# One five-block tile per pair of weight blocks, and a masked bias with the row maximum in one instruction, in a three-branch decoder layer

## The chip, the cores and the metric

One Trainium2 core of eight is used. It has a matrix engine (TensorE, PE in the profile; its weight loads are PEld), VectorE (DVE), ScalarE (ACT), GpSimd (POOL), SyncE (SP), which here only issues transfers, and 16 DMA engines. The metric is the device time of one execution in microseconds.

## The reference

The layer takes x of 512 tokens by 1024 channels, in float32, and computes one mixer with three branches:

```
h = rmsnorm(x) * norm_g;  proj = h @ w_in           # 1024 -> some 14,000 columns, split by name
A: q,k = silu(conv4(aq)), silu(conv4(ak))            # 4 heads of 256, mLSTM with gates ai, af
   yA = rmsnorm(mlstm(q, k, av, ai, af)) * ml_norm_g * sigmoid(ao) * silu(az)
B: 8 heads of 128, forgetting attention:
   F = cumsum(log_sigmoid(bf));  s = q.k/sqrt(128) + F[query] - F[key], -inf above the diagonal
   yB = softmax(s) @ bv * silu(bz)
C: yC = (windowed means of cu (2,4,8,16 tokens) - cu) @ pool_w * pool_scale * silu(cz)
merged = sum over branches of sigmoid(g_n) * (y_n @ w_branch_n)
out = rmsnorm(x + merged @ w_out) * final_g
```

## The kernel before, in words

Every product is made in float32 quality from three passes: a weight or an activation is split into `hi` (a rounded copy, made on ACT, `hi_of`, L288) and `lo` (the rest, made on DVE, `lo_of`, L291), and `mm3` (L300 to L302) adds hi.hi, hi.lo and lo.hi. So each weight block passes through DMA, then ACT, then DVE, before PE can use it.

The weights come in an order written by `plan()`, in two kinds. A **unit** (U) is one block of 128 x 1024 elements (512 KB) and gives 24 matmuls. A **pair** (P) is two blocks of output columns made together by a Strassen-like scheme with seven instead of eight products (`pair`, seven calls of `prod`, 84 matmuls). For a pair, four parts of weights are wanted: part 0 (the two halves of the first block), part 1 (one half of the second), and parts 2 and 3, which are sums of blocks. The first layer head, the first two groups of gates, `av`, `bv`, `pw` (the pool weights), `wb` (branches) and `wo` (output) are units; the rest are pairs.

`feed_pair` of before uses two kinds of raw tiles with two buffers each: R with three plain blocks (768 KB, L370), and T with four blocks, of which two are loaded (512 KB, L375) and then added to in place by an accumulating transfer that POOL issues (L377; 512 KB written); the other two T blocks are sums that DVE makes (L294). R is free once parts 0 and 1 and both sums are made, T after the splits of parts 2 and 3. A unit takes whichever of R and T is free first (`"any"`, in `feed_unit`). Split weights live in four slots, part 1 in a slot of its own (`s3`).

The order of all instructions is settled when the program is written, by a planner (`Flow`) that holds a clock per engine. Each activity (a "chain") is a generator that asks for a buffer (`get`), for another chain's result (`wait`), or for time on an engine; the planner emits what could start by its own costs, near PE's planned time. Transfers are booked with fixed times: 3.4 for a unit, 4.2 for R, 3.4 + 0.9 + 4.2 for T, 2.5 for a bias row. Each engine then runs its instructions in the emitted order and waits on semaphores where data are late; so an instruction whose data come later than booked holds what was emitted behind it on that engine. SP's and POOL's transfers stand in such lines as well.

Attention runs in four couples of heads (`fox_pair`, function `head`). For each head: q and k are split; the negated cumulative forget row is broadcast from DRAM to all 128 partitions into one tile (`nfb`, L1375, single buffer, free after the head's last score); four query blocks of scores of 128, 256, 384 and 512 keys are made on PE; DVE scales them and adds the row (L1400), POOL writes a very negative number above the diagonal (L1404), DVE takes the negated row maximum (L1413), ACT the exponential with its sum (L1421), DVE divides (L1430), PE turns the blocks (L1443). Work tiles `w` are counted: nine for these chains, four per head.

Of the kernel before, what the change touches and what calls it, by code (L numbers as in the profile page):

```python
# [7 lines left out]
F32 = mybir.dt.float32  # L8
F32R = mybir.dt.float32r
AF = mybir.ActivationFunctionType  # L10
ALU = mybir.AluOpType
# [20 lines left out]
PLAIN = 2  # L32

# [55 lines left out]
def v_cost(n):  # L89
    return 0.15 + 1.05e-3 * n  # L90
# [16 lines left out]
class Flow:  # L107
# [39 lines left out]
    def settle(self, c):  # L147

        while c.alive:
            kind = c.req[0]  # L150
            if kind == "get":
                t = self.grab(*c.req[1:])
                if t is None:
                    return False
                self.resume(c, t)
            elif kind == "any":
                names = [n for n in c.req[1] if self.free[n]]
                if not names:
                    return False
                n = min(names, key=lambda n: self.free[n][0])  # L160
                self.resume(c, (n, self.grab(n)))
# [88 lines left out]
def trunk(tc, x, xt_in, w, wpair, cols, fg, out):  # L250
    nc = tc.nc
    with contextlib.ExitStack() as ctx:
# [17 lines left out]
        for name, n in (("R", 2), ("T", 2), ("slot", SLOTS), ("s3", 1), ("C", 5), ("E", 2), ("w", 9),  # L270
                        ("qk", 2), ("v", 1), ("pm", 1), ("em", 1), ("mx", 4), ("pj", 4), ("S", 8),
                        ("f", 2), ("nf", 1)):
            fl.stock(name, n)
# [4 lines left out]
        def work(name, shape=(P, S), dt=F32):  # L278
            return st.tile(list(shape), dt, tag="w", name=name, bufs=11)
# [33 lines left out]
        def raw_tile(tag, name, n):  # L313
            return st.tile([P, n], F32, tag=tag, name=name, bufs=2)
# [11 lines left out]
        def feed_unit(i):  # L326
            what = order[i][1:]
            n = width(what)
            own = what[0] == "pw"
            prio = late(i, 0)  # L330

            def gen():
                if not own:
                    ts = yield ("get", "slot", 1)
                tag, t = yield ("any", ("R", "T"))
                t = yield ("SP", 0.06, t)
                raw = raw_tile(tag, f"raw{i}", n)
# [12 lines left out]
                lo_of(lo, raw, hi)  # L350
                fl.put(tag, 1, t)
                chunks[i, 0] = (hi, lo)
                fl.done["c", i, 0] = t
            fl.add(gen(), prio)

        def feed_pair(i):
            tiles = {}
            src = wpair[index[i]]
            left = {"R": 4, "T": 2}

            def drop(tag, t):
                left[tag] -= 1
                if not left[tag]:
                    fl.put(tag, 1, t)

            def load():
                t = yield ("get", "R", 1)
                t = yield ("SP", 0.06, t)
                r = tiles["R"] = raw_tile("R", f"R{i}", 3 * Q)
                nc.sync.dma_start(out=r, in_=src[:, :3 * Q])  # L370
                fl.done["R", i] = t + 4.2
                t = yield ("get", "T", 1)
                t = yield ("SP", 0.06, t)
                s_ = tiles["T"] = raw_tile("T", f"T{i}", 4 * Q)
                nc.sync.dma_start(out=s_[:, :2 * Q], in_=src[:, :2 * Q])  # L375
                t = yield ("POOL", 0.9, t + 3.4)
                nc.gpsimd.dma_start(out=s_[:, :2 * Q].rearrange("p (a c) -> p a c", a=2),  # L377
                                    in_=src[:, 3 * Q:].unsqueeze(1).to_broadcast([P, 2, Q]),
                                    accum_op=ALU.add)
                fl.done["T", i] = t + 4.2  # L380

            def parts(j, n, name, raw, tag):
                def gen():
                    ts = yield ("get", "s3" if j == 1 else "slot", 1)
                    t = yield ("wait", (tag, i))
                    if j >= 2:
                        if j == 3:
                            t = yield ("wait", ("sum", i))
                        r, s_ = tiles["R"], tiles["T"]
                        t = yield ("DVE", v_cost(Q), t)  # L390
                        if j == 2:
                            add(s_[:, 2 * Q:3 * Q], s_[:, Q:2 * Q], r[:, :Q])
                            fl.done["sum", i] = t
                            drop("R", t)
                        else:
                            add(s_[:, 3 * Q:], s_[:, 2 * Q:3 * Q], r[:, 2 * Q:])
                            drop("R", t)
                    t = yield ("ACT", a_cost(n), max(t, ts))
                    shape = (P, n) if j < 3 else (P, 2, Q)
                    mk = work if j == 1 else b  # L400
                    hi, lo = [mk(f"{x_}{i}_{j}", shape, F32R) for x_ in ("hi", "lo")]
                    hi_of(hi, raw())
                    t = yield ("DVE", v_cost(n), t)
                    lo_of(lo, raw(), hi)
                    drop("R" if j < 2 else "T", t)
# [5 lines left out]
            parts(0, 2 * Q, "s0", lambda: tiles["R"][:, Q:], "R")  # L411
            parts(2, 2 * Q, "a", lambda: tiles["T"][:, Q:3 * Q], "T")
            parts(1, Q, "s3", lambda: tiles["R"][:, :Q], "R")
            parts(3, 2 * Q, "b", lambda: tiles["T"].rearrange("p (a c) -> p a c", a=4)[:, 0::3], "T")

# [32 lines left out]
        def pair(a, c, into, after):  # L448
# [8 lines left out]
            def prod(o, j, half, mov, start, stop, last=False):  # L457
                fl.need(("c", i, j))
                ws = chunks[i, j]
                ws = [(t_[:, half] if j == 3 else t_[:, half * Q:(half + 1) * Q])  # L460
                      .rearrange("p (k c) -> p k c", c=P) for t_ in ws]
# [23 lines left out]
            prod(yz[:, H:], 2, 0, sig["s1"], True, True)  # L485
            side(yz[:, H:], e[:, 2])
            prod(x_[:, :H], 2, 1, sig["s2"], False, True, last=True)
            side(x_[:, :H], e[:, 1], -1.0)
            y4 = bank("y4")
            prod(y4[:, :H], 3, 1, sig["A22"], True, True)  # L490
# [14 lines left out]
            prod(x_[:, :H], 3, 0, sig["s3"], False, True, last=True)  # L505
# [25 lines left out]
        raws = [raw_tile("RRTT"[i], f"raw{i}", D) for i in range(4)]  # L531
# [68 lines left out]
        fill(3, 0, 1)  # L600
# [13 lines left out]
        for name in ("slot", "R", "T"):  # L614
            fl.free[name] = []
# [91 lines left out]
        def gates():  # L707
# [47 lines left out]
            nc.vector.tensor_scalar(out=w_[64:72], in0=csum[64:72], scalar1=-1.0, scalar2=None,  # L755
# [304 lines left out]
        def first_head():  # L1060
# [14 lines left out]
            fl.put("T", 2, 8.0)  # L1075
# [278 lines left out]
        def fox_pair(hp):  # L1354
# [3 lines left out]
            def head(h, cell, t_in):  # L1358
# [13 lines left out]
                tn = yield ("get", "nf", 1)  # L1372
                tn = yield ("SP", 0.06, tn)
# [22 lines left out]
                tm = []  # L1396
                for i in range(NT):
                    n, q0 = (i + 1) * P, i * P
                    t = yield ("DVE", v_cost(n), max(ts[i], tn, tw))
                    nc.vector.scalar_tensor_tensor(out=ss[i][:, :n], in0=os_[i][:, :n], scalar=P ** -0.5,  # L1400
                                                   in1=nf[:, :n], op0=ALU.mult, op1=ALU.add)
                    fl.put("mx", 1, t)
                    t = yield ("POOL", 0.3, t)
                    nc.gpsimd.affine_select(out=ss[i][:, q0:n], in_=ss[i][:, q0:n], pattern=[[-1, P]],  # L1404
                                            compare_op=ALU.is_ge, fill=NEG, base=0, channel_multiplier=1)
                    tm.append(t)
                fl.put("nf", 1, t)
                te, tr = [], []
                ms = []
                for i in range(NT):  # L1410
                    t = yield ("DVE", v_cost((i + 1) * P), tm[i])
                    mxn = sm.tile([P, 1], F32, tag="mxn", name=f"mx{h}{i}", bufs=8)
                    nc.vector.tensor_reduce(out=mxn, in_=ss[i][:, :(i + 1) * P], axis=AX.X, op=ALU.max,  # L1413
                                            negate=True)
                    ms.append((mxn, t))
                es = []
                for i in range(NT):
# [3 lines left out]
                    nc.scalar.activation(out=s_, in_=s_, func=AF.Exp, bias=ms[i][0], accum_out=sme)  # L1421
# [279 lines left out]
def pack(np, w_in, pool_w, w_branch, w_out):  # L1701
# [10 lines left out]
    for it in plan():  # L1712
        if it[0] == "P":
            b1, b2 = [columns(u).transpose(1, 0, 2).reshape(P, 2, Q) for u in it[1:]]
            pairs.append(np.concatenate([b2[:, 1], b1[:, 0], b1[:, 1], b2[:, 0]], axis=1))
# [60 lines left out]
```

## Time and profile before

| | |
|---|---|
| runs | median 889.76 us of three (887.24 to 890.56) |
| profiled execution | 891.74 us; span from first to last instruction 889.8 us |
| PE busy | 854.9 us, 96% of the span |
| DVE / ACT / POOL busy | 625.3 us (70%) / 507.9 us (57%) / 100.8 us (11%) |
| mean granted clock of PE | 0.987 |
| bytes moved | 147.95 MB, mean 166 GB/s |

Read it so: the share of PE is an average over the whole program; what it stands still for is seen only in the waits, place by place. An engine's idle time counts only where PE, or the end, waits for it.

### The profile page before, as it was taken

To read this page: it belongs to the slowest core of one execution; us is meant where nothing else is said; L and a number is where in the kernel's file an instruction comes from. 1 tells how busy PE (TensorE), PEld (TensorE's weight loads), DVE (VectorE), ACT (ScalarE), POOL (GpSimd) and SP (SyncE) were. 2 spreads that over 40 slices of the span, in tenths; PEclk is the share of its full clock that TensorE was granted. 3 is DMA by queue.
4 is the path that set the end of the run, shared out by engine and by line. 5 is a ranking of instruction groups with operands and counts; after the bars stand their busy time and mean duration, and the time that the engine had idled before them with its cause. 6 is when DMAs were issued, how large, how long until landed. Compare 5 with 4: busy or idle time off the path is not lost.

```text
span 889.8 us, 14985 instructions
## 1 busy us (share of the span) xinstructions
PE 854.9 (96%) x5954; PEld 801.6 (90%) x5954; DVE 625.3 (70%) x985; ACT 507.9 (57%) x865; POOL 100.8 (11%) x135
## 2 busy tenths in 40 slices
PE   9999799999999999789899999999998999999997
PEld 7888799999999999689899999999988978888886
DVE  4889799587789668698877686686686763445623
ACT  7569589778687566354556565564565653102313
POOL 0002211111102010011211111211211000000020
PEclk9999899999999999989999999999998999999999
DMA  9326566746655556566556547447556786464302
GB/s 347 108 71 187 141 171 178 190 119 178 186 153 144 171 152 200 135 166 189 168 118 202 157 128 195 131 132 207 149 151 181 264 301 227 163 238 139 96 23 95
DMA packets 48998, 147.95 MB, mean 166 GB/s; under 512 B 4884, under 2 KB 5268, under 8 KB 48928
## 3 DMA queue, kind: packets, MB, share of 16 engines
q1 hardware_dynamic: 36000, 121.19, 38.4%
q0 software_dynamic: 12208, 24.67, 17.4%
q8 instruction: 47, 0.77, 0.4%
q10 hardware_dynamic: 720, 1.13, 0.4%
q14 instruction: 23, 0.19, 0.1%
HBM read 132.26 MB, written 14.70 MB: 165 GB/s over the span
## 4 chain that ended last, share of the span: by engine, by line
PE 59%; DMA 19%; DVE 13%; ACT 4%; issue 4%; SPq 0%; DVEq 0%; POOLq 0%; ACTq 0%
DMA T<-w_pairs 11%; DVE lo L291 6%; PE wb L302 5%; PE wb L301 5%; PE wb L300 5%; DMA raw<-w_units 4%; DMA nfb<-rows 3%; ACT hi L288 3%; PE av L301 2%; PE av L302 2%; PE out L302 2%; PE out L300 2%; PE av L300 2%; PE out L301 2%; DVE T L294 1%
## 5 line engine op out<-in xcount | busy, mean ns | idle before, releaser
L288 ACT CAST hi<-T 128x1024 fp32r<-128x1024 f32 x84 | 88.0, 1048 | 63.9 <-DVE T L294 59.0
L291 DVE TENSOR_TENSOR lo<-T,hi 128x1024 fp32r<-128x1024 f32 x84 | 102.6, 1224 | 15.1 <-ACT hi L288 14.6
L288 ACT CAST hi<-raw 128x1024 fp32r<-128x1024 f32 (+3 forms) x65 | 64.9, 1011 | 84.2 <-DMA raw<-w_units 41.3
L291 DVE TENSOR_TENSOR lo<-raw,hi 128x1024 fp32r<-128x1024 f32 (+3 forms) x65 | 75.7, 1174 | 38.1 <-ACT hi L288 38.0
L377 POOL DMA_DIRECT2D T<-w_pairs x42 | 51.1, 1216 | 436.7 <-DMA T<-w_pairs 187.5
L294 DVE TENSOR_TENSOR T<-T,R 128x512 f32<-128x512 f32 x84 | 58.6, 697 | 39.1 <-DMA T<-w_pairs 34.7
L291 DVE TENSOR_TENSOR lo<-R,hi 128x1024 fp32r<-128x1024 f32 x84 | 80.0, 954 | 5.8 <-ACT hi L288 5.4
L288 ACT CAST hi<-R 128x1024 fp32r<-128x1024 f32 x84 | 69.2, 836 | 0.5 <-DMA R<-w_pairs 0.4
L1601 DVE TENSOR_TENSOR gt<-wb,gt 128x512 f32<-128x512 f32 x16 | 11.1, 692 | 37.3 <-PE wb L302 37.3
L300 PE MATMUL bv<-hi,hT 128*128 128x256 f32 x128 | 36.6, 286 | 0.0
L302 PE MATMUL bv<-hi,hT 128*128 128x256 f32 x128 | 36.2, 282 | 0.0
L301 PE MATMUL bv<-lo,hT 128*128 128x256 f32 x128 | 36.1, 282 | 0.0
L1404 POOL TENSOR_SCALAR_AFFINE_SELECT s<-s 128x128 f32<-128x128 f32 x32 | 20.9, 686 | 81.3 <-DVE s L1400 81.1
L300 PE MATMUL av<-hi,hT 128*128 128x256 f32 x96 | 27.2, 284 | 0.0
L301 PE MATMUL av<-lo,hT 128*128 128x256 f32 x96 | 27.2, 283 | 0.0
L302 PE MATMUL av<-hi,hT 128*128 128x256 f32 x96 | 27.2, 283 | 0.0
L1421 ACT ACTIVATE s<-s,mx 128x128 f32<-128x128 f32 (+3 forms) x32 | 17.9, 563 | 15.7 <-DVE mx L1413 15.7
L288 ACT CAST m<-mg 128x512 fp32r<-128x512 f32 x8 | 5.0, 621 | 38.3 <-DVE mg L294 38.3
L301 PE MATMUL out<-lo,m 128*128 128x512 f32 (+1 forms) x72 | 26.3, 365 | 0.0
L302 PE MATMUL out<-hi,m 128*128 128x512 f32 (+1 forms) x72 | 26.3, 365 | 0.0
L300 PE MATMUL out<-hi,m 128*128 128x512 f32 (+1 forms) x72 | 26.3, 365 | 0.0
L302 PE MATMUL wb<-yc,lo 128*128 128x512 f32 x64 | 24.9, 389 | 0.0
(2187 smaller groups left out, 3338.9 us busy)
## 6 DMA issues: line engine op xcount, KB each, us to landing
R<-w_pairs SPq DMA_DIRECT2D x42, 768.0 KB, 4.5
raw<-w_units SPq DMA_DIRECT2D x58, 512.0 KB, 4.3
T<-w_pairs SPq DMA_DIRECT2D x42, 512.0 KB, 5.1
T<-w_pairs POOLq DMA_DIRECT2D x42, 512.0 KB, 6.6
g<-g SPq DMA_DIRECT2D x12, 512.0 KB, 4.5
yf<-y SPq DMA_DIRECT2D x24, 256.0 KB, 5.5
gt<-g SPq DMA_DIRECT2D x24, 256.0 KB, 4.3
xT<-x_turned SPq DMA_DIRECT2D x8, 256.0 KB, 5.4
```

The costliest lines, as they stand in the source:

```text
L288: nc.scalar.copy(out=hi, in_=full)
L291: nc.vector.tensor_tensor(out=lo, in0=full, in1=hi.bitcast(F32), op=ALU.subtract)
L294: nc.vector.tensor_tensor(out=out_, in0=a, in1=c, op=ALU.add)
L300: nc.tensor.matmul(out_, lhsT=ah, rhs=bh, start=start, stop=False, **kw)
L301: nc.tensor.matmul(out_, lhsT=ah, rhs=bl, start=False, stop=False, **kw)
L302: nc.tensor.matmul(out_, lhsT=al, rhs=bh, start=False, stop=stop, **kw)
L377: nc.gpsimd.dma_start(out=s_[:, :2 * Q].rearrange("p (a c) -> p a c", a=2), in_=src[:, 3 * Q:].unsqueeze(1).to_broadcast([P, 2, Q]), accum ...
L1404: nc.gpsimd.affine_select(out=ss[i][:, q0:n], in_=ss[i][:, q0:n], pattern=[[-1, P]], compare_op=ALU.is_ge, fill=NEG, base=0, channel_multi ...
L1421: nc.scalar.activation(out=s_, in_=s_, func=AF.Exp, bias=ms[i][0], accum_out=sme)
L1601: nc.vector.tensor_tensor(out=g_, in0=o, in1=g_, op=ALU.mult)
```

## The change

A pair gets one raw tile of five blocks; there are three such tiles (`RAWS`), shared by pairs and units, in place of two R and two T. The packing on the host now orders the four blocks of a pair so that blocks 0 and 1 are part 0 and block 2 is part 1. The two blocks that are accumulated into are loaded first, into blocks 3 and 4; then the three plain blocks; then POOL issues the accumulating transfer. DVE's two sums are written over blocks 0 and 1 once part 0 is split (`s0`). The tile is free when all four parts are split. The planner's booked times change with it.

In attention, the bias is broadcast in four pieces, one per query block, into the tile `emat` (which the mLSTM heads use before); POOL masks the pieces, and one DVE instruction adds a piece to the scores, scales by -1/sqrt(128) and takes the row minimum. The exponential then has scale -1. The stored row is scaled by -sqrt(128). Work tiles go from nine to eight.

```diff
-        for name, n in (("R", 2), ("T", 2), ("slot", SLOTS), ... ("w", 9), ... ("nf", 1)):
+        for name, n in (("R", RAWS), ("slot", SLOTS), ... ("w", 8), ...):
...
 feed_unit:
-                tag, t = yield ("any", ("R", "T"))
+                t = yield ("get", "R", 1)
...
                 if own:
+                    yield ("wait", ("av", AH - 1))
                     ts = yield ("get", "v", 1)
-                t = max(t + 3.4, ts)
+                t = max(t + 4.2, ts)
...
 feed_pair, load:
-                r = tiles["R"] = raw_tile("R", f"R{i}", 3 * Q)
-                nc.sync.dma_start(out=r, in_=src[:, :3 * Q])
-                fl.done["R", i] = t + 4.2
-                t = yield ("get", "T", 1)
-                t = yield ("SP", 0.06, t)
-                s_ = tiles["T"] = raw_tile("T", f"T{i}", 4 * Q)
-                nc.sync.dma_start(out=s_[:, :2 * Q], in_=src[:, :2 * Q])
-                t = yield ("POOL", 0.9, t + 3.4)
-                nc.gpsimd.dma_start(out=s_[:, :2 * Q]..., in_=src[:, 3 * Q:]..., accum_op=ALU.add)
-                fl.done["T", i] = t + 4.2
+                r = raw_tile(f"R{i}", 5 * Q)
+                nc.sync.dma_start(out=r[:, 3 * Q:].rearrange("p (a c) -> p a c", a=2),
+                                  in_=src.rearrange("p (a c) -> p a c", c=Q)[:, 0:3:2])
+                t1 = t + 4.5
+                t = yield ("SP", 0.06, t)
+                nc.sync.dma_start(out=r[:, :3 * Q], in_=src[:, :3 * Q])
+                fl.done["R", i] = t + 5.0
+                t = yield ("POOL", 0.9, t1)
+                nc.gpsimd.dma_start(out=r[:, 3 * Q:]..., in_=src[:, 3 * Q:]..., accum_op=ALU.add)
+                fl.done["T", i] = t + 6.2
...
 feed_pair, parts:
-                            add(s_[:, 2 * Q:3 * Q], s_[:, Q:2 * Q], r[:, :Q])
+                            add(r[:, :Q], r[:, 3 * Q:4 * Q], r[:, 2 * Q:3 * Q])
-                            add(s_[:, 3 * Q:], s_[:, 2 * Q:3 * Q], r[:, 2 * Q:])
+                            add(r[:, Q:2 * Q], r[:, :Q], r[:, Q:2 * Q])
...
 start:
-        raws = [raw_tile("RRTT"[i], f"raw{i}", D) for i in range(4)]
+        raws = [raw_tile(f"raw{i}", D) for i in range(RAWS)]
+        def fill_last():
+            raws.append(raw_tile("raw3", D))
+            fill(3, 0, 1)
...
 attention:
-                nf = const.tile([P, S], F32, tag="rB", name=f"nfb{h}")
-                nc.sync.dma_start(out=nf, in_=rows[8 + h:9 + h, :].partition_broadcast(P))
-                tn += 2.5
+                nf_ = st.tile([P, 1280], F32, tag="emat", name=f"nfb{h}", bufs=1)
+                nf = [nf_[:, i * (i + 1) * 64:(i + 1) * (i + 2) * 64] for i in range(NT)]
+                for i in range(NT):
+                    nc.sync.dma_start(out=nf[i],
+                                      in_=rows[8 + h:9 + h, :(i + 1) * P].partition_broadcast(P))
+                tn += 4.0
+                for i in range(NT):
+                    tn = yield ("POOL", 0.5, tn)
+                    nc.gpsimd.affine_select(out=nf[i][:, i * P:], in_=nf[i][:, i * P:], ..., fill=NEG)
...
-                    nc.vector.scalar_tensor_tensor(out=ss[i][:, :n], in0=os_[i][:, :n], scalar=P ** -0.5,
-                                                   in1=nf[:, :n], op0=ALU.mult, op1=ALU.add)
-                    nc.gpsimd.affine_select(out=ss[i][:, q0:n], in_=ss[i][:, q0:n], ..., fill=NEG)
-                    nc.vector.tensor_reduce(out=mxn, in_=ss[i][:, :n], axis=AX.X, op=ALU.max, negate=True)
+                    nc.vector.tensor_tensor_reduce(out=ss[i][:, :n], in0=os_[i][:, :n], in1=nf[i],
+                                                   scale=-P ** -0.5, scalar=-NEG, op0=ALU.add, op1=ALU.min,
+                                                   accum_out=mn)
...
-                    nc.scalar.activation(out=s_, in_=s_, func=AF.Exp, bias=ms[i][0], accum_out=sme)
+                    nc.scalar.activation(out=s_, in_=s_, func=AF.Exp, bias=ms[i][0], scale=-1.0, accum_out=sme)
```

## Rows read from the trace of the kernel before

**Rows 1.** Waits of PE: who waited for whom, us in total, times, longest

```profile
PE cz_cz_5yz L300 <- ACT hi L288: 5.2, 1, 5.2
PE aq_aq_3y L302 <- DVE lo L291: 4.9, 1, 4.9
PE g_g_3y L302 <- DVE lo L291: 4.0, 1, 4.0
PE py L300 <- DVE s L1400: 2.5, 1, 2.5
...
PE tpB L1443 <- DVE s L1400: 1.6, 3, 0.9
PE cu_cu_5yz L302 <- DVE lo L291: 1.5, 1, 1.5
PE g_g_1y L302 <- DVE lo L291: 1.2, 1, 1.2
```

**Rows 2.** Stretches: length, busy time and count per engine, granted clock, DMA share, GB/s

```profile
92.00:104.00 12.00, 7.10 (x45) 6.90 (x44) 8.56 (x11) 6.64 (x10) 1.77 (x3) 0.72 0.34 104
374.00:386.00 12.00, 6.29 (x36) 5.79 (x35) 7.05 (x11) 3.02 (x4) 1.21 (x1) 0.72 0.78 192
675.00:687.00 12.00, 8.02 (x43) 7.69 (x43) 6.88 (x9) 4.20 (x9) 1.20 (x1) 0.72 0.76 260
...
160.00:180.00 20.00, 20.00 (x162) 19.74 (x161) 13.34 (x21) 12.79 (x23) 1.22 (x1) 1.00 0.75 207
```

**Rows 3.** Chain of waits, 80 to 100 us: start, us, what

```profile
76.87 7.45 DMA T<-w_pairs
...
85.00 9.52 DMA T<-w_pairs
```

**Rows 4.** DMA issues of the page: queue, count, KB each, median us to landing

```profile
R<-w_pairs SPq DMA_DIRECT2D x42, 768.0 KB, 4.5
...
T<-w_pairs SPq DMA_DIRECT2D x42, 512.0 KB, 5.1
T<-w_pairs POOLq DMA_DIRECT2D x42, 512.0 KB, 6.6
...
nfb<-rows SPq DMA_DIRECT2D x8, 256.0 KB, 7.1
```

**Rows 5.** Timeline of DVE, 84 to 98 us: start, us, what, idle before

```profile
94.54 0.69 DVE L294 TENSOR_TENSOR T<-T,R 128x512 f32<-128x512 f32 x1 [5.56 <-DMA T<-w_pairs]
```

**Rows 6.** Timelines of SP and DVE, 336 to 380 us

```profile
338.41 0.33 SPq L338 DMA_DIRECT2D raw<-w_units  x1
...
371.29 0.33 SPq L375 DMA_DIRECT2D T<-w_pairs  x1
...
370.04 1.22 DVE L291 TENSOR_TENSOR lo<-raw,hi 128x1024 fp32r<-128x1024 f32 x1
```

**Rows 7.** Timelines of SP, DVE and PE, 8 to 30 us

```profile
9.46 0.33 SPq L536 DMA_DIRECT2D raw<-w_units  x1
...
10.26 0.69 DVE L291 TENSOR_TENSOR lo<-raw,hi 128x512 fp32r<-128x512 f32 x1
...
20.31 1.22 DVE L291 TENSOR_TENSOR lo<-raw,hi 128x1024 fp32r<-128x1024 f32 x1 [0.77 <-ACT hi L288]
...
23.94 0.39 PE L300 MATMUL ak<-hg,hi 128*128 128x512 f32 x1
```

**Rows 8.** Groups of instructions, DVE and ACT: shapes, count, busy us, mean ns

```profile
L1400 DVE SCALAR_TENSOR_TENSOR s<-sB,nfb 128x128 f32<-128x128 f32 (+3 forms) x32 | 15.2, 484 | 8.4 <-DMA nfb<-rows 8.4
L1413 DVE TENSOR_REDUCE mx<-s 128x1 f32<-128x128 f32 (+3 forms) x32 | 13.3, 478 | 0.0
...
L1421 ACT ACTIVATION_READ_ACCUMULATOR s<-s,mx 128x1 f32 x32 | 6.2, 194 | 0.0
```

**Rows 9.** Waits of DVE

```profile
DVE s L1400 <- DMA nfb<-rows: 8.4, 4, 2.9
```

More of the change, by code (lines that the diff above doesn't have):

```diff
@@ L32 @@
 PLAIN = 2
+RAWS = 3
 C_NG = 0
@@ L155, in settle @@
                 self.resume(c, t)
[L156 to L161, printed above, removed]
             elif kind == "wait":
@@ L268, in trunk @@
                 np_ += 1
-        for name, n in (("R", 2), ("T", 2), ("slot", SLOTS), ("s3", 1), ("C", 5), ("E", 2), ("w", 9),
+        for name, n in (("R", RAWS), ("slot", SLOTS), ("s3", 1), ("C", 5), ("E", 2), ("w", 8),
                         ("qk", 2), ("v", 1), ("pm", 1), ("em", 1), ("mx", 4), ("pj", 4), ("S", 8),
-                        ("f", 2), ("nf", 1)):
+                        ("f", 2)):
             fl.stock(name, n)
@@ L278, in work @@
         def work(name, shape=(P, S), dt=F32):
-            return st.tile(list(shape), dt, tag="w", name=name, bufs=11)
+            return st.tile(list(shape), dt, tag="w", name=name, bufs=10)
         def mx(name):
@@ L311, in trunk, with raw_tile @@
         used = [0]
-        def raw_tile(tag, name, n):
-            return st.tile([P, n], F32, tag=tag, name=name, bufs=2)
+        def raw_tile(name, n):
+            return st.tile([P, n], F32, tag="R", name=name, bufs=RAWS)
         at_use, n_ = [], 0
@@ L356, in feed_pair, with blocks @@
         def feed_pair(i):
-            tiles = {}
+            cell = []
             src = wpair[index[i]]
[L359 to L364, printed above, removed]
+            left = [4]
+            def blocks(j):
+                return cell[0].rearrange("p (a c) -> p a c", c=Q)[:, (slice(0, 2), slice(2, 3),
+                                                                     slice(0, 4, 3), slice(1, 5, 3))[j]]
             def load():
@@ L378, in load, with parts @@
+                nc.gpsimd.dma_start(out=r[:, 3 * Q:].rearrange("p (a c) -> p a c", a=2),
                                     in_=src[:, 3 * Q:].unsqueeze(1).to_broadcast([P, 2, Q]),
                                     accum_op=ALU.add)
-                fl.done["T", i] = t + 4.2
-            def parts(j, n, name, raw, tag):
+                fl.done["T", i] = t + 6.2
+            def parts(j, n, key):
                 def gen():
                     ts = yield ("get", "s3" if j == 1 else "slot", 1)
-                    t = yield ("wait", (tag, i))
+                    t = yield ("wait", (key, i))
@@ L386, in gen @@
                     if j >= 2:
[L387 to L390, printed above, removed]
+                        t0 = yield ("wait", ("s0" if j == 2 else "sum", i))
+                        r = cell[0]
+                        t = yield ("DVE", v_cost(Q), max(t, t0))
                         if j == 2:
-                            add(s_[:, 2 * Q:3 * Q], s_[:, Q:2 * Q], r[:, :Q])
+                            add(r[:, :Q], r[:, 3 * Q:4 * Q], r[:, 2 * Q:3 * Q])
@@ L401, in gen @@
                     hi, lo = [mk(f"{x_}{i}_{j}", shape, F32R) for x_ in ("hi", "lo")]
-                    hi_of(hi, raw())
+                    hi_of(hi, blocks(j))
                     t = yield ("DVE", v_cost(n), t)
-                    lo_of(lo, raw(), hi)
-                    drop("R" if j < 2 else "T", t)
+                    lo_of(lo, blocks(j), hi)
+                    if j == 0:
+                        fl.done["s0", i] = t
+                    left[0] -= 1
+                    if not left[0]:
+                        fl.put("R", 1, t)
@@ L410, in feed_pair @@
             fl.add(load(), 0)
[L411 to L414, printed above, removed]
+            parts(0, 2 * Q, "R")
+            parts(2, 2 * Q, "T")
+            parts(1, Q, "R")
+            parts(3, 2 * Q, "T")
         def feed(n):
@@ L459, in prod @@
                 ws = chunks[i, j]
-                ws = [(t_[:, half] if j == 3 else t_[:, half * Q:(half + 1) * Q])
-                      .rearrange("p (k c) -> p k c", c=P) for t_ in ws]
+                ws = [t_[:, half].rearrange("p (k c) -> p k c", c=P) for t_ in ws]
                 for k in range(4):
@@ L484, in pair @@
             prod(yz[:, :H], 0, 1, sig["A12"], True, True, last=True)
-            prod(yz[:, H:], 2, 0, sig["s1"], True, True)
+            prod(yz[:, H:], 2, 1, sig["s1"], True, True)
             side(yz[:, H:], e[:, 2])
-            prod(x_[:, :H], 2, 1, sig["s2"], False, True, last=True)
+            prod(x_[:, :H], 2, 0, sig["s2"], False, True, last=True)
             side(x_[:, :H], e[:, 1], -1.0)
             y4 = bank("y4")
-            prod(y4[:, :H], 3, 1, sig["A22"], True, True)
+            prod(y4[:, :H], 3, 0, sig["A22"], True, True)
             t4 = side(y4[:, :H], e[:, 3])
@@ L504, in pair @@
             fl.put("pj", 1, t)
-            prod(x_[:, :H], 3, 0, sig["s3"], False, True, last=True)
+            prod(x_[:, :H], 3, 1, sig["s3"], False, True, last=True)
             t = fl.now("DVE", v_cost(H))
@@ L599, in trunk @@
         x_load(0)
-        fill(3, 0, 1)
+        fill_last()
         x_load(1)
@@ L613, in trunk @@
         lo_of(dgl, dg, dgh)
-        for name in ("slot", "R", "T"):
+        for name in ("slot", "R"):
             fl.free[name] = []
@@ L754, in gates @@
             t = yield ("DVE", 0.48, t)
-            nc.vector.tensor_scalar(out=w_[64:72], in0=csum[64:72], scalar1=-1.0, scalar2=None,
+            nc.vector.tensor_scalar(out=w_[64:72], in0=csum[64:72], scalar1=-P ** 0.5, scalar2=None,
                                     op0=ALU.mult)
@@ L1371, in head @@
                 fl.put("C", 1, t)
-                tn = yield ("get", "nf", 1)
-                tn = yield ("SP", 0.06, tn)
-                nf = const.tile([P, S], F32, tag="rB", name=f"nfb{h}")
-                nc.sync.dma_start(out=nf, in_=rows[8 + h:9 + h, :].partition_broadcast(P))
-                tn += 2.5
+                tn = yield ("get", "em", 1)
+                tn = yield ("SP", 0.2, tn)
+                nf_ = st.tile([P, 1280], F32, tag="emat", name=f"nfb{h}", bufs=1)
[6 more added lines that the diff above has]
+                    tn = yield ("POOL", 0.5, tn)
+                    nc.gpsimd.affine_select(out=nf[i][:, i * P:], in_=nf[i][:, i * P:], pattern=[[-1, P]],
+                                            compare_op=ALU.is_ge, fill=NEG, base=0, channel_multiplier=1)
                 tw = yield ("get", "w", 4)
@@ L1395, in head @@
                 ss = [work(f"s{h}{i}") for i in range(NT)]
[L1396 to L1399, printed above, removed]
-                    nc.vector.scalar_tensor_tensor(out=ss[i][:, :n], in0=os_[i][:, :n], scalar=P ** -0.5,
-                                                   in1=nf[:, :n], op0=ALU.mult, op1=ALU.add)
[L1402 to L1408, printed above, removed]
                 ms = []
                 for i in range(NT):
[L1411 to L1415, printed above, removed]
+                    n = (i + 1) * P
+                    t = yield ("DVE", v_cost(n) + 0.1, max(ts[i], tn, tw))
+                    mn = sm.tile([P, 1], F32, tag="mxn", name=f"mn{h}{i}", bufs=8)
+                    nc.vector.tensor_tensor_reduce(out=ss[i][:, :n], in0=os_[i][:, :n], in1=nf[i],
+                                                   scale=-P ** -0.5, scalar=-NEG, op0=ALU.add, op1=ALU.min,
+                                                   accum_out=mn)
+                    fl.put("mx", 1, t)
+                    ms.append((mn, t))
+                fl.put("em", 1, t)
                 es = []
@@ L1420, in head @@
                     sme = sm.tile([P, 1], F32, tag="sme", name=f"sm{h}{i}", bufs=8)
-                    nc.scalar.activation(out=s_, in_=s_, func=AF.Exp, bias=ms[i][0], accum_out=sme)
+                    nc.scalar.activation(out=s_, in_=s_, func=AF.Exp, bias=ms[i][0], scale=-1.0,
+                                         accum_out=sme)
                     es.append((sme, t))
@@ L1714, in pack @@
             b1, b2 = [columns(u).transpose(1, 0, 2).reshape(P, 2, Q) for u in it[1:]]
-            pairs.append(np.concatenate([b2[:, 1], b1[:, 0], b1[:, 1], b2[:, 0]], axis=1))
+            pairs.append(np.concatenate([b1[:, 0], b1[:, 1], b2[:, 1], b2[:, 0]], axis=1))
             continue
```

12 lines of the change are left out of this document (5 added, 7 removed).

## The prediction

> **What bounds the kernel now.** I read the page's busy times first, then who waits on TensorE (PE), then stretches around its longest waits with the granted clock, then the chain of waits and the queues' timelines in those stretches. PE is busy for 96% of the span and VectorE (DVE), the next, for 70% (the table above). No matmul is added or removed, so the change can win only PE's standing time and what the clock loses behind it; it can lose by making new standing time.
>
> PE's waits sum to under 30 us; of the eight rows that matter most [rows 1] two families come out.
>
> (a) Weights of a pair. The rows that name the `lo` or `hi` split of a pair (cz 5.2, aq 4.9, g 4.0, cu 1.5, g 1.2) sum to 16.8 us. Behind the first three of them the granted clock falls: each 12 us stretch around one has a mean of 0.72 [rows 2], full speed (2.4 GHz) and a piece at half of it (1.2 GHz), after PE had stood still. The price follows from the counts: in an undisturbed stretch 162 matmuls took 20.00 us, 0.123 each. In the three stretches PE was busy 7.10, 6.29 and 8.02 us for 45, 36 and 43 matmuls, which at 0.123 would be 5.5, 4.4 and 5.3; so 1.6 + 1.9 + 2.7 = 6.2 us are lost to the clock.
>
> (b) Attention scores. py 2.5 and tpB 1.6 wait for the score instruction L1400: 4.1 us.
>
> Why (a) happens: the chain before the aq wait is a load of T (7.45 us) and then the accumulating transfer into it (9.52 us), so 17.6 us from issue to landing [rows 3]. By medians it is 5.1 + 6.6, plus 0.7 from the load's landing to the issue on GpSimd (POOL; 84.32 to 85.00): 12.4 [rows 3, 4]. The planner in the code books T at 3.4 + 0.9 + 4.2 = 8.5 us after its issue. Because it believes that, it puts the sum of pair n+1 into DVE's queue ahead of the last split of pair n. DVE then stood 5.56 us at that sum, with the split that PE needs behind it [rows 5]. The second cause is too few T tiles: the unit `pw` takes one of the two T tiles as its raw buffer at 338.41 and gives it up after the split at 370.04 to 371.26; the next T load goes out at 371.29 [rows 6]. In between all pairs go through one T tile; that is where cu and cz wait.
>
> **The change, part by part.**
>
> 1. *One tile per pair, three tiles.* The same 1.75 MB per pair are moved, by the same three transfers. The T half is now first, the plain three blocks next, and the pair waits for one free tile instead of one R and then one T. Three pairs can be under way, and while `pw` holds a tile, two. A tile is free when all four parts are split, which the one `s3` slot and the four slots allow near the end of the pair before it on PE. A pair is 84 matmuls, 84 x 0.123 = 10.3 us, so a tile freed there is refilled for a pair that starts three pairs (31 us) later, two (21 us) beside `pw`. The chain needs 12.4 us, or 17.6 at its worst; both fit. The planner's figures (4.5 + 0.9 + 6.2 = 11.6 for T) now lie near 12.4, so less is queued ahead of its data. Bounds: all of 16.8 + 6.2 = 23.0 us back, or nothing (a DVE that stands at another sum). I take 20: with the longer lead each of the three clock falls should go, and some 3 us of short waits stay.
>
> 2. *Sums in place.* The sum of part 2 now waits for part 0's `lo`. Behind it on DVE stand other splits; but part 0 rests on the plain load (4.5 [rows 4]), the sum on the accumulate, 12.4 after issue, so `lo` is some 7 us earlier. Cost 0; without that cover one hi and lo, about 2 us per pair. The strided reads of parts 2 and 3 replace one strided and one plain read; counted 0.
>
> 3. *Start: the fourth raw unit shares the first one's tile.* Its load went out at 9.46; now it waits for the first unit's last `lo`, 10.26 + 0.69 = 10.95, so 1.5 us later, with the x loads behind it. Its split ended at 21.53 and PE came to it at 23.94 [rows 7]: 2.4 us of cover. Cost 0; 1 us if the x loads push it further.
>
> 4. *Masked bias and maximum in one instruction.* Per head: one broadcast of 256 KB becomes four of 64 to 256 KB (640 KB), the four selects move from the scores to the bias, ahead of them, and four reduces go. On DVE 32 L1400 (484 ns) and 32 L1413 (478 ns) become 32 fused ones with a [128,1] result [rows 8]. No fused one is in this trace. Its bounds are 484 (an L1400) and 962 (both in turn); I take 484 + 194, the accumulator read of the same scores on ScalarE (ACT), 678. So DVE saves 32 x (962 - 678) = 9 us, between 0 and 15, none of it on PE's path but for (b).
> The Trainium skill says in "VectorE: DVE Perf Modes", section "Two Vector instructions with no wait between them", that an op which also writes out its accumulator is two instructions, the main one and an accumulator read. By it the DVE's count does not fall from 64 to 32, and the 15 us would not be had whole; no run yet shows the read on DVE.
> The path of a head loses a trip through POOL and back. For the second head of a couple the bias tile is freed only by the first head's last score, as before; DVE stood 8.4 us in all there, four times [rows 9], because a broadcast takes 7.1 [rows 4] and 2.5 was booked. Now 4.0 plus 0.6 per select is booked, the real wait ends about where it did or 1 to 3 us later. I take 3 of the 4.1 us of (b); bounds: all 4.1, or 4 us more instead (1 us in each of four couples).
>
> 5. *Small.* Work tiles 9 to 8: two heads hold exactly 8; at worst one py wait, 2.5. 24 more issues on SP of about 0.33 are 8 us spread over 220; SP mostly waits. A reordered queue gives back some waits of the present size: 2 us against me (0 to 8).
>
> Sum: 20 + 3 - 2 = 21. The profiled execution took 891.74 us (span 889.8 and 1.9 around it); 891.74 - 21 = 870.7. The runs' median lies 2.0 below the profiled one, so 868.7: I forecast **869**.
>
> **Rivals.**
>
> *Half of it (877).* Units and pairs now share three tiles, where four stood; in the pool stretch `pw` still sits on one, and there the order keeps DVE at a sum. Then cu 1.5, cz 5.2 and its clock 1.9 stay, and (b) gains nothing: 891.74 - (23.0 - 8.6) + 2 = 879.3, less 2.0 is 877. For it: `pw` held its tile 33 us; against: two whole pairs are left, not one T.
>
> *No change (889).* The transfers were hidden but for the order in the queues, and a new order has as many collisions. For it: PE's waits are only 3% and come at few places. Against: one mechanism carries 16.8 of them.
>
> *Slower: POOL's queue (899).* The accumulating transfers are issued on POOL in order with the bias selects, and a select now waits for its broadcast (6 to 8 us, four of them beside weight loads) where it used to wait for a score. For the second head of each of the four couples the accumulate behind it goes out that much later, and PE stands as at the g row: 4.0 + 2.7 of clock = 6.7. Four times is 26.8; aq, cu and cz still win 4.9 + 1.5 + 5.2 + 1.6 + 1.9 = 15.1; with 2 for order: 891.74 - 15.1 + 26.8 + 2 = 905, less 2 is 903, and 899 where (b) is won all the same. It decides from 15.1/4 = 3.8 us per couple. Against it: pairs have 21 to 31 us of lead for 13.
>
> **How the numbers follow.** Forecast and what lies below it 0.62, half 0.20, no change 0.07, slower 0.11. The lower end: 23.0 + 4.1 and half of the short waits gone, 858. The upper end reaches past the half case, 886, and leaves out the no-change and slower cases. A measurement of this kernel tells about 0.5% (4.4 us) from nothing: faster 0.83, same 0.07, slower 0.10.
>
> **What would show it.** PE's list of waits without the aq, cz and g rows; a granted clock without the three falls; no stand of DVE before a sum like the 5.56. Step 4: a fused instruction near 678 ns with its read, and the second head's score not waiting for a broadcast or select. I am wrong if PE waits long for a split behind an accumulate that POOL issued late, or if a new fall of the clock shows in the attention heads.

## The result, and the profile after

The changed kernel takes 866.08 us (median of four runs, 865.01 to 867.3) where the kernel before takes 888.5 (885.16 to 890.56 in the four runs beside it): a ratio of 0.9752, 95% interval 0.9715 to 0.9788, 22.4 us less. The forecast was 869.

First the page of the kernel after: span, and busy time by engine.

```profile
span 865.5 us, 14996 instructions
...
PE 847.8 (98%) x5954; PEld 797.0 (92%) x5954; DVE 614.4 (71%) x985; ACT 512.9 (59%) x868; POOL 101.2 (12%) x135
```

The span is 24.3 us shorter. PE's busy time fell by 7.1 (854.9 to 847.8) with the same 5954 matmuls; the other 17.2 are standing time. Part of the 7.1 is the clock. PE's busy time in the stretches at half clock (windows: length, then busy time and count by engine), first the sum of the three of before (94.62 to 101.45, 377.93 to 384.76, 678.30 to 685.13), then the only one inside the changed kernel:

```profile
sum 20.49, PE 13.77 PEld 13.48 DVE 17.53 ACT 10.18 POOL 2.62; mean PE 4.59 PEld 4.49 DVE 5.84 ACT 3.39 POOL 0.87
```

```profile
500.93:504.34 3.41, 3.41 (x18) 3.41 (x17) 3.10 (x5) 1.83 (x4) 0.53 (x2) 0.50 0.97 182
```

A matmul of a pair that takes 0.12 us at full clock takes 0.21 at half of it (chain of e3, 470.12 and 489.24), so I estimate that the three falls cost 13.77 x 0.09 / 0.21 = 5.9 us and the new one 1.5. That is 4.4 of the 7.1; what the other 2.7 are these views do not show.

The waits of PE after, longest first, to set beside [rows 1]:

```profile
PE tpB L1444 <- DVE s L1431: 2.4, 2, 1.5
PE aq_aq_7x L295 <- ACT aq_aq_7e L471: 1.9, 1, 1.9
PE ak_ak_3yz L295 <- ACT ak_ak_3e L471: 1.8, 1, 1.8
PE wb L297 <- DVE lo L286: 1.0, 1, 1.0
...
PE aq_aq_3y L297 <- DVE lo L286: 0.8, 1, 0.8
```

cz, cu and g are gone, aq_aq_3y is 0.8 instead of 4.9, and no single wait is longer than 1.9. What is left at aq_aq_7x and ak_ak_3yz waits for copies that ACT makes of results, not for weights. The stretches of [rows 2], after (length, busy time and count by engine, granted clock, DMA share, GB/s):

```profile
92.00:104.00 12.00, 10.44 (x87) 9.88 (x86) 12.00 (x19) 8.59 (x12) 7.62 (x6) 1.00 0.78 184
374.00:386.00 12.00, 12.00 (x102) 12.00 (x101) 11.57 (x18) 7.23 (x13) 2.14 (x4) 1.00 0.95 228
675.00:687.00 12.00, 12.00 (x86) 11.29 (x85) 7.24 (x12) 7.70 (x13) 0.00 (x0) 1.00 0.75 260
```

The granted clock is 1.00 in all three. The group of DVE's sums shows why: its second figure after the bar is the mean of one, its third the time DVE stood before them. Before, and after:

```profile
L294 DVE TENSOR_TENSOR T<-T,R 128x512 f32<-128x512 f32 x84 | 58.6, 697 | 39.1 <-DMA T<-w_pairs 34.7 <-issue 3.9
```

```profile
L289 DVE TENSOR_TENSOR R<-R 128x512 f32<-128x512 f32 x84 | 57.7, 687 | 2.0 <-DMA R<-w_pairs 1.3
```

39.1 us of DVE standing at sums became 2.0. The transfers themselves did not get faster (page, DMA issues: count, KB, median us to landing; against [rows 4]):

```profile
R<-w_pairs SPq DMA_DIRECT2D x42, 768.0 KB, 6.4
...
R<-w_pairs SPq DMA_DIRECT2D x42, 512.0 KB, 4.7
R<-w_pairs POOLq DMA_DIRECT2D x42, 512.0 KB, 6.9
```

They land earlier than they are wanted: from the landing of a pair's accumulating transfer to the start of its first sum the median over the 42 pairs was 3.1 us before and is 13.6 now. And the fused score instruction, which no trace of before had (groups of DVE, after):

```profile
L1410 DVE CUSTOM_DVE_ANT_0 s<-sB,nfb 128x128 f32<-128x128 f32 (+3 forms) x32 | 14.3, 485 | 1.4 <-POOL nfb L1384 1.3
...
L1410 DVE DVE_READ_ACCUMULATOR2_ANT mn<- 128x1 f32 x32 | 2.6, 82 | 0.0
```

485 + 82 = 567 ns, against 484 + 478 for the two that it replaces.

### The profile page after: what moved, and what is told of

It reads as the page before. It is cut to its first block, busy times and chain, and to the rows that moved or that the text cites. A ratio compares the mean times of both kernels' runs of the same rounds, so it can differ in the third digit from the quotient of the medians.

```text
span 865.5 us, 14996 instructions
## 1 busy us (share of the span) xinstructions
PE 847.8 (98%) x5954; PEld 797.0 (92%) x5954; DVE 614.4 (71%) x985; ACT 512.9 (59%) x868; POOL 101.2 (12%) x135
## 4 chain that ended last, share of the span: by engine, by line
PE 72%; DMA 11%; ACT 7%; DVE 6%; issue 1%; SPq 1%; POOL 0%; DVEq 0%; ACTq 0%; POOLq 0%
PE wb L297 4%; PE wb L296 4%; PE wb L295 4%; DMA raw<-w_units 4%; DMA nmb<-rows 3%; DVE lo L286 2%; ACT hi L283 2%; PE out L297 2%; PE out L296 2%; PE out L295 2%; DMA R<-w_pairs 2%; PE av L296 1%; PE av L297 1%; PE av L295 1%; PE bv L296 1%
## 5 line engine op out<-in xcount | busy, mean ns | idle before, releaser
L286 DVE TENSOR_TENSOR lo<-R,hi 128x1024 fp32r<-128x1024 f32 (+1 forms) x168 | 180.7, 1086 | 46.3 <-ACT hi L283 45.9
L283 ACT CAST hi<-R 128x1024 fp32r<-128x1024 f32 (+1 forms) x168 | 155.1, 944 | 40.1 <-DVE R L289 31.7
L375 POOL DMA_DIRECT2D R<-w_pairs x42 | 51.1, 1216 | 336.0 <-DMA R<-w_pairs 158.2
L289 DVE TENSOR_TENSOR R<-R 128x512 f32<-128x512 f32 x84 | 57.7, 687 | 2.0 <-DMA R<-w_pairs 1.3
L296 PE MATMUL wb<-yc,hi 128*128 128x512 f32 x64 | 24.9, 389 | 0.0
L295 PE MATMUL wb<-yc,hi 128*128 128x512 f32 x64 | 24.9, 389 | 0.0
L295 PEld LDWEIGHTS bv<-hi,hT 128*128 128x128 f32 x128 | 24.5, 191 | 0.3
L296 PEld LDWEIGHTS bv<-lo,hT 128*128 128x128 f32 x128 | 24.5, 191 | 0.2
```

The costliest lines, as they stand in the source:

```text
L283: nc.scalar.copy(out=hi, in_=full)
L286: nc.vector.tensor_tensor(out=lo, in0=full, in1=hi.bitcast(F32), op=ALU.subtract)
L289: nc.vector.tensor_tensor(out=out_, in0=a, in1=c, op=ALU.add)
L295: nc.tensor.matmul(out_, lhsT=ah, rhs=bh, start=start, stop=False, **kw)
L296: nc.tensor.matmul(out_, lhsT=ah, rhs=bl, start=False, stop=False, **kw)
L375: nc.gpsimd.dma_start(out=r[:, 3 * Q:].rearrange("p (a c) -> p a c", a=2), in_=src[:, 3 * Q:].unsqueeze(1).to_broadcast([P, 2, Q]), accum_ ...
```

## The experiments

Runs 1 to 4 shared a chip and its runs of the kernel before (887.62), so did 5 to 8 (887.87) and 9 to 12 (885.17). Small differences are compared within such a group.

**e1: the tiles alone.** From the changed kernel, the attention part of the diff is undone (work tiles stay at eight).

```diff
-                tn = yield ("get", "em", 1)  ... four broadcasts, four selects, tensor_tensor_reduce
+                tn = yield ("get", "nf", 1)  ... one broadcast, scalar_tensor_tensor, select, tensor_reduce
```

> The five-block tile and the booked times of the change, with the attention of before (one plain bias row, mask on GpSimd after the score, a separate maximum). Theory (weights): the gain is the weights' chain, so 22 us less 2 to 3 for the scores: 868 to 870, PE without the waits on aq, cu, cz and g and with waits on py/tpB of 2 to 4 us. Rival (attention): the selects that stood between two score instructions held GpSimd's line of accumulating transfers, and freeing it is the gain: 880 or more.

865.02 us (862.62 to 865.33), ratio 0.9726 (0.967 to 0.9781). The whole gain is here, a little more of it than the theory gave. PE's waits on py and tpB are 0.4 and 2.0, against 2.5 and 1.6 before, though the attention is the old one.

**e2: the attention alone.** The kernel before with that part of the diff put in, and nothing else (work tiles stay at nine).

```diff
-                tn = yield ("get", "nf", 1)  ... one broadcast, scalar_tensor_tensor, select, tensor_reduce
+                tn = yield ("get", "em", 1)  ... four broadcasts, four selects, tensor_tensor_reduce
```

> The attention of the change (masked bias, one instruction for score and maximum) on the two R and two T tiles and the booked times of before. Theory (weights): 884 to 887, the three falls of the clock still there. Rival (attention): 875 or less. If both edits are worth something only together, neither this run nor the tile alone comes near 866.

893.44 us, ratio 1.0061 (1.0022 to 1.0101): 0.6% slower, which neither theory expected. An order alone moves the kernel by 0.5% (e8), so the time shows that the attention alone wins nothing, and not that it costs. The trace, of an execution of 899.31 us, shows one way in which it can cost. PE's longest wait, and its chain of waits from 632 to 652 us (start, us, what):

```profile
PE tpB L1442 <- DVE mn L1408: 8.2, 4, 3.5
```

```profile
636.92 12.45 DMA T<-w_pairs
...
650.00 0.28 DVE s L1408
```

An accumulating transfer issued while the four broadcasts were on their way took 12.45 us, not 6.6; DVE stood 3.58 at its sum, and the scores stood behind that sum in DVE's line, though their bias was masked at 644.14:

```profile
649.39 0.69 DVE L294 TENSOR_TENSOR T<-T,R 128x512 f32<-128x512 f32 x1 [3.58 <-DMA T<-w_pairs]
650.00 0.28 DVE L1408 CUSTOM_DVE_ANT_0 s<-sB,nfb 128x128 f32<-128x128 f32 x1
```

**e3: the changed kernel with the booked times of before.**

```diff
-                t = max(t + 4.2, ts)          # unit
+                t = max(t + 3.4, ts)
-                t1 = t + 4.5
+                t1 = t + 3.4
-                fl.done["R", i] = t + 5.0
+                fl.done["R", i] = t + 4.2
-                fl.done["T", i] = t + 6.2
+                fl.done["T", i] = t + 4.2
```

> The changed kernel, but with the booked transfer times of before (unit 3.4, plain blocks 4.2, accumulated blocks 3.4 + 0.9 + 4.2). Theory (lead): with three tiles the data are there anyway; 866 to 870. Rival (booking): the sums are again queued ahead of their data, DVE stands at them, and half or more of the gain goes: 876 to 886.

877.43 us, ratio 0.9869 (0.9814 to 0.9924) against 0.9752 for the changed kernel: nearly half of the gain is lost. But not at the sums, whose data land 14.9 us ahead of them (median). The group of sums of e3, and PE's longest waits:

```profile
L289 DVE TENSOR_TENSOR R<-R 128x512 f32<-128x512 f32 x84 | 57.8, 688 | 2.3 <-DMA R<-w_pairs 1.4
```

```profile
PE bq_bk_3x L295 <- ACT bq_bk_3e L473: 4.4, 1, 4.4
PE bq_bk_7x L295 <- ACT bq_bk_7e L473: 3.2, 1, 3.2
```

PE waits for a copy that ACT makes of a result (`side` in `pair`), and the chain of waits shows what ACT stood at:

```profile
476.87 10.34 DMA raw<-w_units
...
487.28 1.04 ACT hi L283
488.32 0.29 ACT bq_bk_3e L473
488.62 0.04 issue
488.66 0.58 PE bq_bk_3x L295
```

A unit's load behind a pair's loads and four broadcasts took 10.34 us; booked at 3.4, its split had been put into ACT's line ahead of the copy. In the changed kernel the same load is as late (10.95), but there the copy stands ahead of the split (timeline of ACT):

```profile
480.77 0.38 ACT L473 ACTIVATE bq_bk_3e<-bq_bk_3x 128x256 f32<-128x256 f32 x1
488.17 1.05 ACT L283 CAST hi<-raw 128x1024 fp32r<-128x1024 f32 x1 [7.02 <-DMA raw<-w_units]
```

The three waits of this kind in e3 (4.4, 3.2 and 1.8, at bq_bk_5x) are the long ones that the changed kernel has not, and all lie among the attention's broadcasts.

**e4: the kernel before with the booked times of the change.**

```diff
-                t = max(t + 3.4, ts)          # unit
+                t = max(t + 4.2, ts)
-                fl.done["R", i] = t + 4.2
+                fl.done["R", i] = t + 5.0
-                t = yield ("POOL", 0.9, t + 3.4)
+                t = yield ("POOL", 0.9, t + 4.5)
-                fl.done["T", i] = t + 4.2
+                fl.done["T", i] = t + 6.2
```

> The kernel before, with nothing but the booked transfer times of the change (unit 4.2, plain blocks 5.0, accumulated blocks 4.5 + 0.9 + 6.2). Theory (lead): the tiles are still too few, pw still holds one T for some 30 us; the cz wait stays, 880 to 887. Rival (booking): the order of DVE's line was all that was wrong: 866 to 874.

876.87 us, ratio 0.9872 (0.9802 to 0.9942), between the two answers. The sums of e4:

```profile
L294 DVE TENSOR_TENSOR T<-T,R 128x512 f32<-128x512 f32 x84 | 58.1, 691 | 16.4 <-DMA T<-w_pairs 16.1
```

DVE's standing at the sums fell from 39.1 to 16.4, and the wait at cz_cz_5yz from 5.2 to 1.7, though `pw` takes its tile as before. The sums still come only 3.3 us after the landing (median), so the lead is the tiles' work and not the times'.

What each is worth can be read in two ways, since e3 has the new attention and e1 and e4 have the old one. With the old attention: 887.6 before, the times alone 876.9 (e4), tiles and times 865.0 (e1), so 11 us for the times and 12 for the tiles on top. With the new one, by ratio: 1.0061 (e2), the tiles 0.9869 (e3), tiles and times 0.9752 (the changed kernel), so some 17 us for the tiles and 10 for the times on top. So the times are worth 10 to 11 us and the tiles 12 to 17, and each of these figures can be off by the some 4 us that a mere change of order makes (e8). New tiles and old times with the old attention were not run; without the four broadcasts the old times may cost less there.

**e5: masked bias, but two instructions for score and maximum.**

```diff
-                    nc.vector.tensor_tensor_reduce(..., op0=ALU.add, op1=ALU.min, accum_out=mn)
+                    nc.vector.scalar_tensor_tensor(out=ss, in0=os_, scalar=P ** -0.5, in1=nf[i], ...)
+                    nc.vector.tensor_reduce(out=mn, in_=ss, axis=AX.X, op=ALU.max, negate=True)
```

> The changed kernel with its masked bias, but score and maximum as two DVE instructions again (a plain scale-and-add, then a row maximum). Theory (the fused instruction saves DVE time that nobody waits for): DVE busy up by about 10 us, time 865 to 868. Rival (it shortens a path PE waits on): 870 or more, with longer waits of PE on tpB.

865.56 us, ratio 0.9732 (0.9687 to 0.9777). DVE's busy time is 626.5 us against 614.4: the fused instruction saves DVE 12.1 us, and nobody waits for them.

**e6: one broadcast per head.**

```diff
+                nfp = const.tile([P, S], F32, tag="rB", name=f"nfp{h}")
+                nc.sync.dma_start(out=nfp, in_=rows[8 + h:9 + h, :].partition_broadcast(P))
-                for i in range(NT):
-                    nc.sync.dma_start(out=nf[i], in_=rows[8 + h:9 + h, :(i + 1) * P].partition_broadcast(P))
-                    nc.gpsimd.affine_select(out=nf[i][:, i * P:], in_=nf[i][:, i * P:], ...)
+                    nc.gpsimd.affine_select(out=nf[i], in_=nfp[:, :(i + 1) * P], ..., base=i * P)
```

> The changed kernel with one broadcast of 256 KB per head into the old bias tile instead of four (640 KB); GpSimd's four selects read it and write the four masked pieces, up to 512 wide. Theory (the four broadcasts load the DMA engines and make neighbouring accumulating transfers late, 13 us instead of 7): the accumulates next to them land in about 7, and the time is 1 to 4 us lower, 862 to 865. Rival (that lateness is hidden by the three tiles): 865 to 868, no difference.

863.18 us (861.94 to 863.75), ratio 0.9712 (0.9676 to 0.9748); against e5 in the same group (863.09 to 866.67) it is lower by 2.4 with ranges that just touch. e12, which is e6 but for one booked time, has the changed kernel's ratio, so a gain in time is not shown. The mechanism does show: accumulates beside one couple's broadcasts, first in the changed kernel (543 to 560 us), then in e6 (539 to 555 us), median of two:

```profile
R<-w_pairs POOLq DMA_DIRECT2D x2, 512.0 KB, 10.4
```

```profile
R<-w_pairs POOLq DMA_DIRECT2D x2, 512.0 KB, 7.1
```

and POOL's wait for the broadcasts, changed kernel and e6:

```profile
POOL nfb L1384 <- DMA nfb<-rows: 53.5, 25, 7.4
```

```profile
POOL nfb L1383 <- DMA nfp<-rows: 27.7, 6, 7.1
```

PE's waits on tpB are gone in e6, and the trace shows where the longest of them (1.5) came from in the changed kernel. Its chain of waits from 472 to 502 us begins at the late load of a unit:

```profile
477.20 10.95 DMA raw<-w_units
488.15 0.02 issue
488.17 1.05 ACT hi L283
489.23 0.02 issue
489.25 0.83 DVE lo L286
...
500.60 1.48 PE tpB L1444 x7
```

The scores stood behind that unit's split in DVE's line and began at 492.86, though their bias was masked at 487.25 and PE had made the last of them at 488.24. In e6 the same load, behind one broadcast, took 6.5 instead of 11.0, and the scores began at 487.86. Most of the lateness had been hidden by the three tiles; what could be won was at most the rest.

**e7: the pool-weight unit takes its raw tile late, in the kernel before.**

```diff
+                if own:
+                    yield ("wait", ("av", AH - 1))
+                    ts = yield ("get", "v", 1)
                 tag, t = yield ("any", ("R", "T"))
...
-                if own:
-                    ts = yield ("get", "v", 1)
```

> The kernel before, with one thing moved: the pool-weight unit takes its raw tile only when its place for the split weights is free, so it no longer holds a T tile for 30 us. Theory (too few T tiles there): the waits on cu and cz and their fall of the clock go, 8.6 us: 878 to 881. Rival (only the order of DVE's line counts): 885 to 889, the waits stay or move.

882.6 us (873.61 to 887.61), ratio 0.9932 (0.99 to 0.9964): 5.3 us, short of the 8.6 expected, and by e8 not safely more than a change of order gives. In the trace, which is of the shortest execution (873.61), the long cz wait is gone (1.4 is left), a g wait of 3.8 and a py wait of 3.1 stand. What the tile held by `pw` costs by itself stays open: e4 took most of the cz wait away without touching it.

**e8: another order alone, in the kernel before.**

```diff
-LOOK = 1.0
+LOOK = 1.05
```

> The kernel before with the planner's look-ahead at 1.05 instead of 1.0: nothing but another order of the same instructions. Theory (the order of before is an ordinary one): within 4 us of before, with its falls of the clock at about the same places. Rival (before is an unlucky order): 875 or less.

883.58 us, ratio 0.995 (0.9926 to 0.9973): 4.3 us from order alone, with its waits moved:

```profile
PE py L300 <- DVE s L1400: 3.4, 1, 3.4
PE cz_cz_5yz L300 <- ACT hi L288: 3.0, 1, 3.0
PE ao_ao_5y L302 <- DVE lo L291: 2.2, 1, 2.2
```

The expectation that its falls of the clock stay at about the same places missed: they begin at 151, 379 and 437 us, before at 95, 378 and 678. So an edit that moves this kernel by 0.5% proves nothing of its own cause. The differences that e1, e3 and e4 show lie well above that.

**e9: another order alone, in the changed kernel** (the same edit as e8).

> The changed kernel with the planner's look-ahead at 1.05 instead of 1.0: nothing but another order. Theory (three tiles and true booked times make the order matter little): 863 to 869. Rival (the change hit a lucky order): 873 or more.

867.37 us, ratio 0.9784 (0.9746 to 0.9823): the gain does not hang on one lucky order.

**e10: the plain blocks loaded first.** The two loads of a pair change places, with their booked times (plain blocks 4.5, accumulated half 5.0).

```diff
-                nc.sync.dma_start(out=r[:, 3 * Q:]..., in_=src...[:, 0:3:2])
                 nc.sync.dma_start(out=r[:, :3 * Q], in_=src[:, :3 * Q])
+                nc.sync.dma_start(out=r[:, 3 * Q:]..., in_=src...[:, 0:3:2])
```

> The changed kernel with the three plain blocks loaded before the two that are accumulated into, as the kernel before did, and booked so. Theory (with three tiles the order of a pair's two loads is hidden): 865 to 868. Rival (issuing the accumulated half first is part of the gain): 870 or more, with waits of PE on the splits of parts 2 and 3.

862.96 us (861.98 to 866.71), ratio 0.9753 (0.9716 to 0.979). The ratio is that of the changed kernel (0.9752): the order of the two loads is hidden.

**e11: e6 with pair transfers booked as measured.**

```diff
-                t1 = t + 4.5
+                t1 = t + 5.2
-                fl.done["R", i] = t + 5.0
+                fl.done["R", i] = t + 6.0
-                fl.done["T", i] = t + 6.2
+                fl.done["T", i] = t + 7.0
```

> The single broadcast of e6, with pair transfers booked as they were measured there: 5.2 for the accumulated half's load, 6.0 for the plain blocks, 0.9 + 7.0 for the accumulate. Theory (booking too little is what is left at the pair rows): 860 to 862. Rival (what is left is DVE and ACT work, not data): 862 to 866.

859.99 us (859.0 to 861.24), ratio 0.9712 (0.9681 to 0.9743), the shortest of all and clear of e9, e10 and e12 on the same chip; against the changed kernel itself it can be set only by the ratio, whose interval overlaps. It lies 4.2 us below e12, its nearest kin, which is what a change of order alone can do (e8); so that the true times did it is not shown. PE's longest waits:

```profile
PE ak_ak_3yz L295 <- ACT ak_ak_3e L471: 1.8, 1, 1.8
PE warm_ps L556 <- POOL ones L549: 1.0, 1, 1.0
PE aq_aq_3y L297 <- DVE lo L286: 0.9, 1, 0.9
```

**e12: e6 with the bias row booked at 7.0.**

```diff
-                tn += 4.0
+                tn += 7.0
```

> The single broadcast of e6 with the bias row booked at 7.0 instead of 4.0 (measured 5.7, at most 7.8). Theory (nothing waits for the row any more): 862 to 865. Rival: 861 or less, if a score still stood in DVE's line before its row.

864.22 us (862.59 to 865.04), ratio 0.9757 (0.9727 to 0.9788): nothing waits for the row.

## Why the prediction was right, and where it was not

**The total.** 21 us were forecast and 22.4 came, and part of that nearness is luck: by e1's ratio the tiles brought some 4 more than was taken for them, and the attention none of the 3 that it was given.

**Step 1, the tiles: right in mechanism, small in size, incomplete in cause.** 20 were forecast out of at most 23.0; e1 brought 24 by its ratio (887.62 x (1 - 0.9726), interval 19 to 29) without the attention. The five rows went and with them the three falls, which by their stretches cost some 5.9 us, near the 6.2 worked out from counts. That both too few tiles and too small booked times were at work was in the prediction; e3 and e4 show both, the times with 10 to 11 us. Wrong was where the booked times act on the changed kernel. They were to matter at the sums; in e3 DVE stands only 2.3 us at all sums, so three tiles cure these by themselves, and what true times add there is at ACT, where a unit's split no longer stands ahead of PE's copies. Waits of PE for such copies were in the trace of before too (bq_bk_5yz 1.7), and the prediction's two families leave them out. e3 set back the pair's and the unit's times together, so that the unit's figure alone does it is read from its chain, not tried alone.

**Step 2, sums in place: right.** DVE stands 2.0 us before 84 sums; 1.3 of them for data, so the wait for part 0 costs next to nothing. **Step 3, the start: right.** The fourth unit's split ended at 21.40 us, before at 21.53. (PE's wait on av, which grew from 0.3 to 1.0, is at another unit, at 42 us.)

**Step 4, the attention: wrong.** "I take 3 of the 4.1 us of (b)": no gain is to be seen. The changed kernel and e1 cannot be told apart (ratios 0.9752 and 0.9726), and e2 alone is no faster than before. The tiles by themselves had brought (b) from 4.1 to 2.4 (e1), and the new attention leaves it at 2.4. The fused instruction was even cheaper than taken, 567 ns instead of 678. On the Trainium skill's rule, that an op which writes out its accumulator is two instructions ("VectorE: DVE Perf Modes", "Two Vector instructions with no wait between them"), the trace agrees: 32 reads of 82 ns beside 32 main ones, and DVE's count stays 985. But the saving lies off PE's path (e5), and what the step left out is the price of the transfers. The four broadcasts make accumulates beside them land at 10.4 instead of 7.1 and a unit's load at 11.0 instead of 6.5 (e6), so the scores come no sooner: they stand behind that unit's split, or, with two T tiles, behind a late sum (e2). py 2.5 and tpB 1.6 became tpB 2.4. One of the prediction's own signs of being wrong came true here: a new fall of the clock in the attention heads, 3.41 us from 500.93 on, behind the tpB wait of 1.5.

**Step 5: right in kind.** Order alone moves this kernel by up to 4 us (e8), and e9 lies within 3 us of the changed kernel by its ratio.

**The rivals.** *Half of it* fell: with three shared tiles cu and cz do not wait. *No change* fell. *Slower* had part of a true mechanism: accumulates do land late beside the broadcasts, in the changed kernel too. These landings are counted from POOL's issue, so what lengthens them is the load on the transfers and not POOL's line. The lead of three tiles covers it, as its "against" said; with two T tiles the trace of e2 shows PE waiting behind it.

## What to carry to other kernels

Where a planner fixes the order of several engines' lines, a transfer that is booked too short puts its consumer ahead of work that others wait for: book what the trace shows, and look for an engine that stands at a first wait with ready work behind it. One kind of tile for all users, taken once, gave the lead that hid transfers of 12 us and more. A buffer that is taken before its user can run is one buffer less for as long; what that cost here by itself e7 leaves open. Fewer instructions on an engine that PE does not wait for bought nothing here, and the transfers that came with the fusion were not free.

## What the runs showed of the hardware that was not expected

Broadcasts of a row to 128 partitions can make their neighbours late. With four per head (640 KB) beside weight loads, the seven accumulating transfers of 512 KB that overlapped one took 9.6 to 13.3 us in the changed kernel; with one per head (256 KB) the seven of e6 took 6.4 to 7.7. Whether the bytes or the number of transfers does it no run separates, and an accumulate can be late without them: in the changed kernel five of those that met no broadcast took 9.7 to 10.8 us.

The falls of the granted clock are not all of one length, and the length of a stand alone does not tell whether one follows: the three of before held 6.83 us each, around stands of 4.9, 5.2 and 4.0 us; the one inside the changed kernel held 3.41, after a stand of 1.5, while its stands of 1.8 (ak_ak_3yz) and 1.9 (aq_aq_7x) had none behind them.
